# A branch ahead of expert 0, small loads in the first mixer, a shorter routing chain and MLP products on the unscaled residual

## The chip, the cores and the metric

One core of a Trainium2 chip runs one launch. The metric is the device time of that launch in microseconds, the median of several runs. Engines are called PE (TensorE), DVE (VectorE), ACT (ScalarE), POOL (GpSimd) and SP (the sync engine, which issues the DMAs of the weights).

## What is computed

256 tokens of 1024 features go through two blocks, all in float32. The first block is a gMLP and HGRN2 mixer and a mixture of 32 experts with two per token. The second block is modulated by a condition vector (12 modulation vectors of 1024, from `w_ada`), and holds an attention, an MLP, a differential attention and a second MLP.

```python
def first_block(x, ...):
    n1 = rms_norm(h, norm1_gain[l]); proj = n1 @ w_in[l]
    ...
    h = h + jnp.concatenate([a_out, b_out], axis=-1) @ w_out[l]
    n2 = rms_norm(h, norm2_gain[l])
    h = h + hier_moe(n2, ...)         # top-1 of 4 groups, then top-2 of its 8 experts
    return rms_norm(h, final_gain)
# an expert: silu(xb @ w_gate[e]) * (xb @ w_up[e]), times w_down[e]

def second_block(x, c, ...):
    cond = jax.nn.silu(c)
    for i in range(2):
        sh1, sc1, g1, sh2, sc2, g2 = jnp.split(cond @ w_ada[i] + b_ada[i], 6, axis=-1)
        h = rms_norm_2(x, ln_mix_g[i]) * (1.0 + sc1) + sh1
        y = nsa_mixer(h, ...) if i == 0 else diff_mixer(h, ...)
        x = x + g1 * y
        h = rms_norm_2(x, ln_mlp_g[i]) * (1.0 + sc2) + sh2
        x = x + g2 * (jnp.square(jax.nn.relu(h @ w_mlp_in[i])) @ w_mlp_out[i])
    return x
```

## The kernel before

Activations stay in SBUF, features on partitions: `res` is `[128, 8, 256]`. Weights stream once from HBM in tiles of 1 MB that SP issues in a fixed order through a ring of buffers; during the experts 18 tiles are in flight. An SP issue waits until the buffer that it fills has been read for the last time, and everything behind it on SP waits too. Outside the experts a float32 product is three passes of matmuls over a high and a low part (`passes`); for each half of a weight tile ACT writes the high part `whi` (L147) and DVE the low part `wlo` (L148). A scheduler orders the instructions of each engine by its own cost estimates, so that the order in the program is only loosely the order on an engine.

**Routing.** After the first mixer `lps` (the router's products) and `yps` (the tokens in natural layout, for the gather) come off PE. A chain of some twenty short DVE instructions yields the choice of experts `sel` (L1080), PE counts ranks from it (`pps`, L1107), DVE makes a one-hot matrix (`hot`, L1267), and PE gathers the tokens of the first four experts with it (`gps`, L1284). `natural` (L1083) writes the high and low parts of the natural tokens: for the first half of the features ACT writes the high part and a copy, and POOL subtracts (L1095); for the second half DVE does the low part behind the one-hot (L1098). Meanwhile PE works on tiles of `w_ada` (`adaps`, L183). `rint` (L1141) says how many tokens did not fit an expert's 64 slots; `past_slots` (L1186 to L1189) loads it into a register of each engine and branches over the block that handles them, which these inputs skip. It is called after expert 5.

**Experts.** Each is `gups` (gate and up, L1330), `htps`, `dps` (down, L1360), and `sums` (L1378) for two at a time. At e == 8 the program builds tables for the second block (L1434 to L1566), with 13 small DMAs on SP: `posi`, five `rg`, two `w`, `bgate`, and four `lv`.

**MLPs.** `out_late` ends the attention before: its `closing` (L476) adds four pairs of `olate` banks to `res`, and `Stats` (L285) counts squares on PE (`ssps`), 1 / rms follows through POOL (`rs_r`, L282) and is spread over partitions (`rbps`). `modulated` then writes the normalized, modulated `hT_hi` and `hT_lo` (L352 to L359); tiles of `w_ada` fill PE's waits there. `mlp` (L1658) runs nine steps j; PE does `hp` (96 matmuls of the first product) of step j and `mlp` (96 of the second) of the step before. `ada_vector` (L252, L254) does tiles of `w_ada` on DVE instead, two instructions a tile, 12 tiles during MLP 0.

Of the kernel before, what the change touches and what calls it, by code (L numbers as in the profile page):

```python
# [13 lines left out]
F32 = mybir.dt.float32  # L14
# [12 lines left out]
T = 256  # L27
D = 1024
# [9 lines left out]
BORROW = 13  # L38
IDLE = 8
# [3 lines left out]
def block_kernel(ctx: ExitStack, tc: tile.TileContext, A: dict, out: bass.AP):  # L43
# [21 lines left out]
    hT_hi = const.tile([P, KD, T], F32R, name="hT_hi")  # L65
    hT_lo = const.tile([P, KD, T], F32R, name="hT_lo")

# [5 lines left out]
    ones = const.tile([P, P], F32, name="ones")  # L73
# [211 lines left out]
    class Stats:  # L285


        def __init__(self, weights=None):
            self.w = weights
            self.q = {}  # L290
            self.tiles = None
# [10 lines left out]
        def square(self, pr, v):  # L302
            q = sc((P, 2, T), name="sq")
            self.q[pr] = q
            if pr == KD // 2 - 1 and self.w is None:
# [4 lines left out]
            if pr == KD // 2 - 1:  # L310
                hold(act=ins)
            if self.w is None:
                nc.vector.tensor_tensor(q[:, 0, :], q[:, 0, :], q[:, 1, :], op=ALU.add)

        def count(self, pr):
# [3 lines left out]
            n = 1 if self.w is None and pr < KD // 2 - 1 else 2  # L319
# [11 lines left out]
        def rstd(self):  # L331
# [7 lines left out]
            return rb[:, 0:T]  # L339

# [38 lines left out]


# [9 lines left out]
    def proj_T_steps(w, c0, outs, n=512, cut=1):  # L390

        for k0, t in colblock(w, c0, n, cut):
            for k1, hi, lo in halves(t):
                for kk in range(hi.shape[1]):
                    k = k0 + k1 + kk
                    for h in range(n // P):
                        for i, (a, b) in enumerate(passes((hi, lo), (hT_hi, hT_lo))):
# [5 lines left out]
                                stop=(k == KD - 1 and i == 2 and h % 2 == 1),  # L403
                            )
# [71 lines left out]
    def closing(banks, gate=None, st=None, each=None):  # L476
# [62 lines left out]
    def out_late(w, r0, got, gate=None, st=None, each=None):  # L539
# [4 lines left out]
        rows(w, r0 // P + 2, banks, got(2), 2, False, closing(banks, gate, st, each))  # L544
# [49 lines left out]
    with tc.tile_pool(name="pa", bufs=1, reuse_waits="tile") as pa:  # L594
# [90 lines left out]
        for h in range(2):  # L685
            small_loads.append(
                (g2[:, 4 * h : 4 * h + 4], A["norm2_gain"][:, h * 512 : (h + 1) * 512].rearrange("o (p k) -> (o p) k", k=4))
            )
        fT = [acc((P, 2, T), name="fT") for _ in range(2)]
# [316 lines left out]
    with (  # L1006
# [78 lines left out]
        def natural(h, behind=None):  # L1085
            s = slice(h * 512, (h + 1) * 512)
            for m in range(2):
# [3 lines left out]
                nc.scalar.activation(hi, ps, AF.Copy, scale=r2[:, m : m + 1])  # L1091
                if behind is None:
                    y = sc((P, 4, P), name="y")
                    nc.scalar.activation(y, ps, AF.Copy, scale=r2[:, m : m + 1])
                    nc.gpsimd.tensor_tensor(lo, y, hi.bitcast(F32), op=ALU.subtract)  # L1095
                else:
                    with tc.issue_after(behind.ins):
                        nc.vector.scalar_tensor_tensor(  # L1098
                            lo, ps, r2[:, m : m + 1], hi.bitcast(F32), op0=ALU.mult, op1=ALU.subtract
                        )  # L1100

        natural(0)
# [1162 lines left out]
```

## Time and profile before

| | |
|---|---|
| median of three runs | 1322.52 us (1319.78 to 1324.54) |
| profiled execution | 1326.57 us, of which the span from first to last instruction is 1324.8 |
| PE busy | 1279.0 us of the span |
| DVE, ACT, POOL busy | 637.6, 494.1, 72.2 us |
| mean granted clock of PE | 0.987 |

The span falls into the first mixer (to about 131 us), routing (to 148), experts (to about 611), the second block's attention (to 796), MLP 0 (to about 992), the differential attention (to 1127) and MLP 1. In the experts the DMA engines are busy throughout; in the rest it is PE. A view by windows gives for each stretch PE's granted clock as a share of full speed, the DMA engines' busy share and what they moved.

### The profile page before, as it was taken

To read this page: it belongs to the slowest core of one execution; us is meant where nothing else is said; L and a number is where in the kernel's file an instruction comes from. 1 tells how busy PE (TensorE), PEld (TensorE's weight loads), DVE (VectorE), ACT (ScalarE), POOL (GpSimd) and SP (SyncE) were. 2 spreads that over 40 slices of the span, in tenths; PEclk is the share of its full clock that TensorE was granted. 3 is DMA by queue.
4 is the path that set the end of the run, shared out by engine and by line. 5 is a ranking of instruction groups with operands and counts; after the bars stand their busy time and mean duration, and the time that the engine had idled before them with its cause. 6 is when DMAs were issued, how large, how long until landed. Compare 5 with 4: busy or idle time off the path is not lost.

```text
span 1324.8 us, 22820 instructions
## 1 busy us (share of the span) xinstructions
PE 1279.0 (97%) x9551; PEld 1010.1 (76%) x9551; DVE 637.6 (48%) x1172; ACT 494.1 (37%) x856; POOL 72.2 (5%) x95
## 2 busy tenths in 40 slices
PE   8999898999999999999999999999999999999998
PEld 7779565665555555556886688999997779999998
DVE  6865410131101111005786768667557677655554
ACT  6643310121101111004455644444445554544543
POOL 1010100000000000000410000000001220000000
PEclk9999899999999999998998999999999999999999
DMA  8997799899999999999545838688558432755520
GB/s 279 397 371 274 303 420 417 316 386 419 420 418 419 420 419 419 419 418 333 200 162 189 313 96 325 225 287 307 180 179 278 147 116 96 262 184 191 181 75 33
DMA packets 99157, 373.98 MB, mean 282 GB/s; under 512 B 10650, under 2 KB 14443, under 8 KB 74731
## 3 DMA queue, kind: packets, MB, share of 16 engines
q1 hardware_dynamic: 99050, 372.49, 74.2%
q8 instruction: 77, 1.26, 0.4%
q14 instruction: 30, 0.24, 0.0%
HBM read 371.41 MB, written 1.05 MB: 281 GB/s over the span
## 4 chain that ended last, share of the span: by engine, by line
PE 66%; issue 13%; DVE 2%; DMA 1%; ACT 1%; POOL 1%; POOLq 0%; DVEq 0%; ACTq 0%
PE mlp L441 14%; PE hp L398 13%; PE gups L1330 9%; PE dps L419 5%; PE dps L1360 4%; PE sums L1378 2%; PE oearly L527 2%; PE qp L419 2%; PE gps L1284 2%; PE adaps L183 2%; PE kv L419 1%; PE opair L2028 1%; PE kcv L419 1%; PE ptps L2019 1%; PE olate L441 1%
## 5 line engine op out<-in xcount | busy, mean ns | idle before, releaser
L148 DVE TENSOR_TENSOR wlo<-w,whi 128x1024 fp32r<-128x1024 f32 (+1 forms) x222 | 270.1, 1218 | 173.5 <-ACT whi L147 172.3
L147 ACT CAST whi<-w 128x1024 fp32r<-128x1024 f32 (+1 forms) x222 | 230.5, 1043 | 246.6 <-PE mlp L441 80.2
L1330 PE MATMUL gups<-w,xg 128*64 128x256 f32 x2048 | 236.4, 385 | 3.4 <-PEq L1189 3.4
L1330 PEld LDWEIGHTS gups<-w,xg 128*64 128x64 f32 x2048 | 145.5, 138 | 92.1 <-issue 25.9
L441 PE MATMUL mlp<-hid,whi 128*128 128x256 f32 x1024 | 183.9, 282 | 0.0
L441 PEld LDWEIGHTS mlp<-hid,whi 128*128 128x128 f32 x1024 | 156.8, 188 | 1.2 <-issue 1.2
L398 PE MATMUL hp<-hT_lo,whi 128*128 128x256 f32 x512 | 143.5, 283 | 1.1 <-DVE hT_lo L359 1.0
L441 PE MATMUL mlp<-hid,wlo 128*128 128x256 f32 x512 | 142.7, 282 | 0.0
L398 PE MATMUL hp<-hT_hi,wlo 128*128 128x256 f32 x512 | 141.4, 282 | 0.0
L398 PE MATMUL hp<-hT_hi,whi 128*128 128x256 f32 x512 | 140.7, 282 | 0.0
L1342 DVE TENSOR_TENSOR h<-h,gups 128x256 f32<-128x256 f32 x32 | 13.5, 422 | 248.8 <-ACT h L1341 248.8
L1360 PE MATMUL dps<-w,hT 128*64 128x512 f32 x496 | 113.2, 596 | 6.1 <-ACT hT L1350 5.0
L398 PEld LDWEIGHTS hp<-hT_lo,whi 128*128 128x128 f32 x512 | 96.0, 188 | 1.5 <-DVE hT_lo L359 1.4
L398 PEld LDWEIGHTS hp<-hT_hi,whi 128*128 128x128 f32 x512 | 95.4, 189 | 0.8 <-ACT hT_hi L358 0.8
L441 PEld LDWEIGHTS mlp<-hid,wlo 128*128 128x128 f32 x512 | 95.9, 188 | 0.0
L398 PEld LDWEIGHTS hp<-hT_hi,wlo 128*128 128x128 f32 x512 | 95.5, 188 | 0.0
L1360 PEld LDWEIGHTS dps<-w,hT 128*64 128x64 f32 x496 | 33.9, 137 | 65.7 <-issue 53.3
L1341 ACT ACTIVATE h<-gups 128x256 f32<-128x256 f32 x32 | 12.3, 383 | 179.4 <-PE gups L1330 179.4
L1371 DVE COPY ysb<-dps 64x512 f32<-64x512 f32 x31 | 21.2, 683 | 108.2 <-PE dps L1360 108.1
L1372 ACT COPY ysb<-dps 64x512 f32<-64x512 f32 x31 | 18.0, 581 | 140.0 <-DVE ysb L1371 140.0
L1378 PE MATMUL sums<-sw,ysb 128*128 128x256 f32 x256 | 61.5, 385 | 6.3 <-DVE ysb L1371 6.3
L282 POOL TENSOR_TENSOR rs_r<-rs_t,mhalf 128x8 f32<-128x8 f32 (+2 forms) x24 | 37.4, 1562 | 480.9 <-DVE rs_t L276 475.9
(529 smaller groups left out, 2019.1 us busy)
## 6 DMA issues: line engine op xcount, KB each, us to landing
w<-in_w_gate_dram SPq DMA_DIRECT2D x64, 1024.0 KB
w<-in_w_up_dram SPq DMA_DIRECT2D x64, 1024.0 KB
w<-in_w_down_dram SPq DMA_DIRECT2D x62, 1024.0 KB
w<-in_w_ada_dram SPq DMA_DIRECT2D x48, 1024.0 KB
w<-in_w_mlp_in_dram SPq DMA_DIRECT2D x32, 1024.0 KB
w<-in_w_mlp_out_dram SPq DMA_DIRECT2D x32, 1024.0 KB
w<-in_diff_w_in_dram SPq DMA_DIRECT2D x12, 1024.0 KB
w<-in_w_in_dram SPq DMA_DIRECT2D x10, 1024.0 KB
```

The source lines that it names most:

```text
L147: nc.scalar.copy(hi, v)
L148: nc.vector.tensor_tensor(lo, v, hi.bitcast(F32), op=ALU.subtract)
L183: nc.tensor.matmul(ps[32 * j : 32 * j + 32, :], lhsT, w[:, j * T : (j + 1) * T], start=start, stop=stop)
L282: nc.gpsimd.tensor_tensor(r, t, m, op=ALU.pow)
L398: nc.tensor.matmul(outs[h // 2][:, h % 2, :], a[:, kk, h * P : (h + 1) * P], b[:, k, :], start=(k == 0 and i == 0 and h % 2 == 0), stop=(k ...
L419: nc.tensor.matmul(outs[m], b[:, k, m * P : (m + 1) * P], a[:, kk, :], start=(k == 0 and i == 0), stop=(k == KD - 1 and i == 2),)
L441: nc.tensor.matmul(outs[dc // 2][:, dc % 2, :], a[:, 0, dc * P : (dc + 1) * P], b[:, a0 + kk, :], start=(first and kk == 0 and i == 0 and ...
L527: nc.tensor.matmul(banks[h // 2][:, h % 2, :], a[:, kk, h * P : (h + 1) * P], b[:, k, :], start=(k == 0 and i == 0 and h % 2 == 0), stop=( ...
L1284: nc.tensor.matmul(ps[:, j, :], part[:, m, k * P : (k + 1) * P], hot[:, m].rearrange("p e s -> p (e s)"), start=(n == 0), stop=(n == 3),)
L1330: nc.tensor.matmul(ps[j * 64 : (j + 1) * 64, s * 256 : (s + 1) * 256], xg[:, k, s0 : s0 + SLOTS], w[k // 4][:, k % 4, j * 256 : (j + 1) * ...
L1360: nc.tensor.matmul(dps[half * 64 : (half + 1) * 64, :], hT[:, c, j * 64 : (j + 1) * 64], dt[f // 2][:, f % 2, half * 512 : (half + 1) * 51 ...
L1378: nc.tensor.matmul(sums[k // 2][:, k % 2, :], t[:, k * P : (k + 1) * P], sw, start=(pr == 0 and k % 2 == 0), stop=(after is not None and k ...
```

## The change

Four parts. (1) `past_slots()` is called ahead of expert 0, and `weigh(0)` after the first products of expert 0. (2) Nine of the small loads go to the first mixer's list of small loads, and the four of `lv` with their four small instructions behind `out_late` of the second block's attention; the mask `cmask` is held once. (3) All high parts of the natural tokens are written first, on ACT, all low parts on DVE behind the one-hot; five bf16 matmuls of 128x512 whose result nobody reads run on PE ahead of `pps` and three behind. (4) The MLPs' first products run on `res * gain` without 1 / rms, written in `closing` pair by pair; a column 256 holds the shift, so that its product is the bias; each result takes 1 / rms (`rb`, the same for all partitions) and bias afterwards. `hp` is now four banks of 258 columns a step. Of the 36 tiles of `w_ada` on PE eight go to DVE, which does vectors 6 to 10.

```diff
@@ Stats
+        def scale(self):
+
+            r = rstd_of(self.ps[:, :, 0], D, "n")
+            rb = mm(name="rbps")
+            spread(r, rb[:, 0:T])
+            t = small.tile([P, T], F32, tag="nf", name="rb", bufs=3)
+            nc.scalar.copy(t, rb[:, 0:T])
+            return t
...
+    def feeding(gain, bias):
+
+        hi, lo = hX
+        for t in hX:
+            nc.vector.memset(t.bitcast(F32)[:, :, T + 1 : TX], 0.0)
+        b = bias[:, :, None]
+        nc.vector.tensor_copy(hi[:, :, T : T + 1], b)
+        nc.vector.tensor_tensor(lo[:, :, T : T + 1], b, hi[:, :, T : T + 1].bitcast(F32), op=ALU.subtract)
+
+        def feed(pr):
+            for k in (2 * pr, 2 * pr + 1):
+                g = gain[:, k : k + 1]
+                nc.scalar.activation(hi[:, k, 0:T], res[:, k, :], AF.Copy, scale=g)
+                nc.vector.scalar_tensor_tensor(
+                    lo[:, k, 0:T], res[:, k, :], g, hi[:, k, 0:T].bitcast(F32), op0=ALU.mult, op1=ALU.subtract
+                )
+
+        return feed
...
+    def proj_X_steps(w, c0, outs):
+
+        for k0, t in colblock(w, c0, 512):
+            for k1, hi, lo in halves(t):
+                for kk in range(hi.shape[1]):
+                    k = k0 + k1 + kk
+                    for h in range(4):
+                        for i, (a, b) in enumerate(passes((hi, lo), hX)):
+                            nc.tensor.matmul(
+                                outs[h],
+                                a[:, kk, h * P : (h + 1) * P],
+                                b[:, k, :],
...
@@ closing
+            if feed is not None:
+                feed(pr)
+                st.square(pr, v)
+                if pr >= 2:
+                    st.count(pr - 2)
+                return
...
@@ first mixer
+        posi = const.tile([P, 2], I32, name="posi")
+        small_loads.append((posi, A["positions_2"].rearrange("o (m p) -> p (o m)", p=P)))
...
+            small_loads.append((rope_gains[:, i, :], g[:, 0:16].to_broadcast([P, 16])))
...
@@ routing
-        natural(0)
+        for h in range(2):
+            natural(h, "high")
         for _ in range(2):
             ada_half([route["last"]])
+
+        unread = mm(name="unread")
+
+        def busy(n):
+            for _ in range(n):
+                nc.tensor.matmul(
+                    unread, onesb, onesb[:, None, :].to_broadcast([P, 4, P]), start=True, stop=True
+                )
+
+        with tc.manual_schedule(engines={mybir.EngineType.PE}):
+            busy(WAIT)
...
+        with tc.issue_after(ranked.ins):
+            busy(3)
...
             if q4 == 0:
-                natural(1, one_hot)
+                for h in range(2):
+                    natural(h, "low", one_hot)
...
         wt, rint = token_weights()
-        weigh(0, hot0)
+        past_slots()
...
                 h, silu, prod = gate_up(e)
+                if e == 0:
+                    weigh(0, hot0)
...
-            if e == 5:
-                past_slots()
...
@@ mlp
-                hp = [mm((P, 2, T), name="hp") for _ in range(2)]
-                proj_T(w_i, j * 512, hp)
+                hp = [(mm if j else acc)((P, TX), name="hp") for _ in range(4)]
+                for n, _ in enumerate(proj_X_steps(w_i, j * 512, hp)):
+                    if j == 0 and n == 3:
+                        st.count(2)
+                        st.count(3)
+                        rb = st.scale()
...
-                    nc.scalar.activation(r, hp[i], AF.Relu)
+                    b = pw.tile([P, 4], F32, tag="nm", name="hb")
+                    for c in range(2):
+                        nc.vector.tensor_copy(b[:, c : c + 1], hp[2 * i + c][:, T : T + 1])
+                        nc.vector.tensor_tensor(r[:, c, :], hp[2 * i + c][:, 0:T], rb, op=ALU.mult)
+                        nc.scalar.activation(r[:, c, :], r[:, c, :], AF.Relu, bias=b[:, c : c + 1])
...
-                    nc.vector.tensor_tensor(r, r, r, op=ALU.mult)
+                    nc.scalar.activation(r, r, AF.Square)
...
-                if ada_at[0] < vectors:
-                    ada_vector(ada_sum)
+                for _ in range(2):
+                    if j and ada_at[0] < vectors:
+                        ada_vector(ada_sum)
...
@@ second block, after the first mixer
-    out_late(w_o, 512, late, mods[2], st)
-    modulated(st, 0, 3, col("lnm", 0, 8))
-    st = Stats()
-    mlp(0, lambda banks: closing(banks, mods[5], st), 10)
+    st_x = Stats(plain=True)
+    out_late(w_o, 512, late, mods[2], st_x, feed=feeding(*modulation(0, 3, col("lnm", 0, 8))))
...
+        nc.sync.dma_start(lv[:, i, :], A[f"diff_{nme}_2"].to_broadcast([P, 64]))
...
+    mlp(0, lambda banks: closing(banks, mods[5], st), st_x, 11)
```

The order of instructions, at three places. First PE between the gather for the first four experts and expert 0. Before:

```order
L1284 MATMUL gps<-hot,hT_lo 128x256 x3
L1284 MATMUL gps<-hot,hT_hi 128x256 x2
L1284 MATMUL gps<-hot,hT_lo 128x256 x2
L1137 MATMUL rps<-ident,rmx 1x128
L1313 MATMUL wps<-ident,hw 128x128 x4
L1330 MATMUL gups<-w,xg 64x256 x64
L1348 MATMUL htps<-ident,h 128x128 x2
L1360 MATMUL dps<-w,hT 64x512 x8
```

After, up to the branch, and then from behind the skipped block:

```order
L1367 MATMUL gps<-hot,hT_lo 128x256 x2
L1219 MATMUL rps<-ident,rmx 1x128
L1270 TENSOR_LOAD rint
L1271 COMPARE_AND_BRANCH
L358 MATMUL rbps<-ident,rs_r 128x128 x2
L1287 COMPARE_AND_BRANCH
L1287 UNCONDITIONAL_BRANCH x2
L2342 BRANCH_PREFETCH_HINT
```

```order
L1287 UNCONDITIONAL_BRANCH
L1271 UNCONDITIONAL_BRANCH
L1413 MATMUL gups<-w,xg 64x256 x32
L1396 MATMUL wps<-ident,hw 128x128 x4
L1413 MATMUL gups<-w,xg 64x256 x32
L1431 MATMUL htps<-ident,h 128x128 x2
L1443 MATMUL dps<-w,hT 64x512 x8
```

Behind `rps` PE now loads the register and branches, and the `wps` of `weigh(0)` stand after the first half of `gups`.

Second, SP's queue. Before, behind the skipped block (its end is the first three rows) in the experts:

```order
L1189 UNCONDITIONAL_BRANCH
L127 DMA w<-in_w_down_dram 128x2048
L1453 DMA posi<-in_positions_dram 128x2x1
L1483 DMA rg<-in_nsa_q_gain_dram 128x16
L1483 DMA rg<-in_nsa_k_gain_dram 128x16 x2
L1483 DMA rg<-in_diff_q_gain_dram 128x16
L1516 DMA w_2646<-in_nsa_w_ck_2_dram 128x64
L1517 DMA w_2646<-in_nsa_w_cv_2_dram 128x64
L1560 DMA bgate<-in_nsa_b_gate_dram 128x48
L127 DMA w<-in_w_gate_dram 128x2048 x2
L127 DMA w<-in_w_up_dram 128x2048 x2
```

After, in the first mixer, and behind the skipped block, which now ends ahead of most of the experts' loads:

```order
L105 DMA g_107<-in_norm_gain_dram 128x4 x2
L105 DMA posi<-in_positions_dram 128x2x1
L105 DMA rope_gains<-in_nsa_q_gain_dram 128x16
L105 DMA rope_gains<-in_nsa_k_gain_dram 128x16 x2
L105 DMA rope_gains<-in_diff_q_gain_dram 128x16
L105 DMA rope_gains<-in_diff_k_gain_dram 128x16
L105 DMA w_200<-in_nsa_w_ck_2_dram 128x64
L105 DMA w_200<-in_nsa_w_cv_2_dram 128x64
L105 DMA bgate<-in_nsa_b_gate_dram 128x48
L131 DMA w<-in_w_in_dram 128x4x512 x2
L131 DMA w<-in_w_ada_dram 128x2x1024 x2
L131 DMA w<-in_w_in_dram 128x4x512 x2
```

```order
L1287 UNCONDITIONAL_BRANCH
L1271 UNCONDITIONAL_BRANCH
L1270 ISA x2
L131 DMA w<-in_w_up_dram 128x2048 x2
L131 DMA w<-in_w_down_dram 128x2048 x2
L131 DMA w<-in_w_gate_dram 128x2048 x2
L131 DMA w<-in_w_up_dram 128x2048 x2
```

The small loads stand in front of the first mixer's weights instead of the experts' weights.

Third, PE where the second block's attention ends and MLP 0 begins. Before:

```order
L441 MATMUL olate<-oT,whi 128x256 x2
L441 MATMUL olate<-oT,wlo 128x256
L323 MATMUL ssps<-ones,sq 128x1 x4
L183 MATMUL adaps<-w,cond 32x256 x8
L323 MATMUL ssps<-ones,sq 128x1 x4
L183 MATMUL adaps<-w,cond 32x256 x8
L344 MATMUL rbps<-ident,rs_r 128x128 x2
L183 MATMUL adaps<-w,cond 32x256 x16
L398 MATMUL hp<-hT_hi,whi 128x256 x2
L398 MATMUL hp<-hT_lo,whi 128x256
```

After:

```order
L448 MATMUL hp<-hT_hi,whi 128x258 x2
L328 MATMUL ssps<-ones,sq 128x1 x4
L491 MATMUL olate<-oT,whi 128x256 x2
L491 MATMUL olate<-oT,wlo 128x256
L491 MATMUL olate<-oT,whi 128x256 x2
L491 MATMUL olate<-oT,wlo 128x256
L491 MATMUL olate<-oT,whi 128x256 x2
L491 MATMUL olate<-oT,wlo 128x256
L491 MATMUL olate<-oT,whi 128x256 x2
L491 MATMUL olate<-oT,wlo 128x256
L448 MATMUL hp<-hT_lo,whi 128x258
L448 MATMUL hp<-hT_hi,wlo 128x258
```

The `adaps` and the wait for `rbps` between the last `olate` and `hp` are gone; `hp` begins while `olate` still runs.

## Rows read from the trace of the kernel before

**Rows 1.** Windows: length, busy us of PE, PEld, DVE, ACT, POOL; clock, DMA share, GB/s.

```profile
90.00:135.00 45.00, 43.18 (x359) 38.76 (x358) 25.05 (x42) 13.59 (x22) 3.20 (x8) 1.00 0.70 265
...
140.00:145.00 5.00, 4.21 (x20) 4.24 (x21) 3.59 (x13) 0.47 (x1) 0.00 (x0) 0.50 0.97 406
145.00:150.00 5.00, 4.83 (x35) 3.89 (x36) 3.08 (x10) 2.71 (x4) 1.66 (x2) 0.83 0.00 0
...
235.00:250.00 15.00, 14.49 (x116) 9.68 (x113) 4.38 (x10) 3.23 (x7) 1.04 (x1) 1.00 0.58 198
285.00:295.00 10.00, 10.00 (x90) 7.49 (x87) 2.04 (x4) 1.92 (x4) 0.00 (x0) 1.00 0.79 310
300.00:580.00 280.00, 272.43 (x1916) 158.89 (x1912) 34.51 (x70) 35.22 (x76) 3.12 (x3) 1.00 1.01 419
```

**Rows 2.** Chain that ended last, 220 to 300 us: start, us, what.

```profile
226.02 10.10 PE gups L1330 x64
236.11 4.03 PE gps L1284 x32
...
244.96 6.91 PE gups L1330 x64
```

**Rows 3.** Line view of the branch, L1189: duration ns min/median/max, start us; who waited.

```profile
L1189 PEldq COMPARE_BRANCH  x1: 6006/6006/6006, 219.6 to 219.6; - x1
...
  PE gups L1330: 3.4, 1
```

**Rows 4.** SP's waits, 215 to 245 us: total us, times, longest.

```profile
SPq L1189 <- SPq L1189: 14.5, 2, 12.0
```

**Rows 5.** Timeline, routing to expert 0: start us, us, instruction [idle before <-releaser].

```profile
137.81 1.26 POOL L1095 TENSOR_TENSOR hT_lo<-y,hT_hi 128x512 fp32r<-128x512 f32 x1
137.98 1.31 DVE L1070 TENSOR_TENSOR hot<-iota,eidx 128x64 f32<-128x64 f32 x2
...
139.69 0.20 PE L1107 MATMUL pps<-sel,lower 128*128 128x32 bf16 x2 [2.56 <-DVE sel L1080]
140.79 1.41 PE L1284 MATMUL gps<-hot,hT_hi 128*128 128x256 f32 x5 [0.87 <-DVE hot L1267]
140.89 1.40 DVE L1098 SCALAR_TENSOR_TENSOR hT_lo<-yps,rs_r,hT_hi 128x512 fp32r<-128x512 f32 x2
...
148.33 3.03 PE L1330 MATMUL gups<-w,xg 128*64 128x256 f32 x26
148.41 0.13 DVE L1141 CAST rint<-rtop 1x1 int32<-1x1 f32 x1
150.32 0.33 SPq L127 DMA_DIRECT2D w<-in_w_up_dram  x1
```

**Rows 6.** Timeline of SP at the small loads among the experts.

```profile
239.59 0.83 SPq L1483 DMA_DIRECT2D rg<-in_nsa_k_gain_dram  x2
```

**Rows 7.** Timeline of PE around the starts of the two MLPs.

```profile
796.46 0.95 PE L323 MATMUL ssps<-ones,sq 128*128 128x1 f32 x8
...
1126.95 0.95 PE L323 MATMUL ssps<-ones,sq 128*128 128x1 f32 x8
```

**Rows 8.** Chain that ended last, in the MLPs.

```profile
829.22 11.39 PE mlp L441 x96
840.62 11.50 PE hp L398 x96
...
1134.39 23.24 PE hp L398 x192
```

**Rows 9.** Groups by form, 796 to 1010 us: busy us, mean ns, idle before.

```profile
L254 DVE SCALAR_TENSOR_TENSOR adasum<-w,cond,adasum 128x1024 f32<-128x1024 f32 x20 | 25.6, 1280 | 1.9 <-DMA w<-in_w_ada_dram 1.9
L183 PE MATMUL adaps<-adasum,ones 128*32 128x256 f32 x24 | 1.9, 391 | 0.0
```

**Rows 10.** Windows in MLP 0, with columns as in Rows 1.

```profile
900.00:920.00 20.00, 20.00 (x170) 20.00 (x170) 19.48 (x20) 8.21 (x11) 0.00 (x0) 1.00 0.90 324
920.00:940.00 20.00, 20.00 (x170) 20.00 (x169) 10.91 (x11) 9.48 (x11) 0.00 (x0) 1.00 0.72 251
```

More of the change, by code (lines that the diff above doesn't have):

```diff
@@ L27 @@
 T = 256
+TX = T + 2
 D = 1024
@@ L38 @@
 BORROW = 13
+WAIT = 5
 IDLE = 8
@@ L64, in block_kernel @@
     res = const.tile([P, KD, T], F32, name="res")
-    hT_hi = const.tile([P, KD, T], F32R, name="hT_hi")
-    hT_lo = const.tile([P, KD, T], F32R, name="hT_lo")
+    hT = [const.tile([P, KD * TX], F32R, name=f"hT_{n}") for n in ("hi", "lo")]
+    hT_hi, hT_lo = (t[:, : KD * T].rearrange("p (k t) -> p k t", t=T) for t in hT)
+    hX = [t.rearrange("p (k t) -> p k t", t=TX) for t in hT]
     ident = const.tile([P, P], F32, name="ident")
@@ L72, in block_kernel @@
     nc.vector.memset(mhalf, -0.5)
-    ones = const.tile([P, P], F32, name="ones")
+    ones = const.tile([P, 32], F32, name="ones")
     nc.vector.memset(ones, 1.0)
@@ L285, in block_kernel, with __init__ @@
     class Stats:
-        def __init__(self, weights=None):
+        def __init__(self, weights=None, plain=False):
             self.w = weights
+            self.plain = plain
             self.q = {}
@@ L304, in square @@
             self.q[pr] = q
-            if pr == KD // 2 - 1 and self.w is None:
+            if pr == KD // 2 - 1 and self.w is None and not self.plain:
                 for j in range(2):
@@ L309, in square @@
             ins = nc.scalar.activation(q, v, AF.Square)
-            if pr == KD // 2 - 1:
+            if pr == KD // 2 - 1 and not self.plain:
                 hold(act=ins)
-            if self.w is None:
+            if self.w is None and not self.plain:
                 nc.vector.tensor_tensor(q[:, 0, :], q[:, 0, :], q[:, 1, :], op=ALU.add)
@@ L318, in count @@
             q = self.q.pop(pr)
-            n = 1 if self.w is None and pr < KD // 2 - 1 else 2
+            n = 1 if self.w is None and pr < KD // 2 - 1 and not self.plain else 2
             for j in range(n):
@@ L403, in proj_T_steps @@
                                 stop=(k == KD - 1 and i == 2 and h % 2 == 1),
+                            )
+                    yield
+    def proj_X_steps(w, c0, outs):
[9 more added lines that the diff above has]
+                                b[:, k, :],
+                                start=(k == 0 and i == 0),
+                                stop=(k == KD - 1 and i == 2),
                             )
@@ L543, in out_late @@
         rows(w, r0 // P, banks, got(0), 0, True)
-        rows(w, r0 // P + 2, banks, got(2), 2, False, closing(banks, gate, st, each))
+        rows(w, r0 // P + 2, banks, got(2), 2, False, closing(banks, gate, st, each, feed))
     class Chains:
@@ L1083, in block_kernel, with natural @@
         y_lo = hT_lo.rearrange("p k t -> p (k t)").rearrange("p (m d) -> p m d", m=2)
-        def natural(h, behind=None):
+        def natural(h, part, behind=None):
             s = slice(h * 512, (h + 1) * 512)
@@ L1108, in block_kernel @@
             if m == 1:
-                nc.tensor.matmul(pps[:, m, 0:NE], onesb, sel[:, 0, :], start=False, stop=True)
+                ranked = nc.tensor.matmul(pps[:, m, 0:NE], onesb, sel[:, 0, :], start=False, stop=True)
+        with tc.issue_after(ranked.ins):
+            busy(3)
         rank = bt("rank", (P, 2, NE))
@@ L1656, in weights_T, with mlp @@
         return t
-    def mlp(lay, close, vectors=0):
-        if vectors:
-            ada_sum = ct("adasum", (P, D), tag="klo")
-            if ada_at[1]:
-                ada_half()
+    def mlp(lay, close, st, vectors):
+        ada_sum = ct("adasum", (P, D), tag="klo")
+        if ada_at[1]:
+            ada_half()
         w_i, w_o = A["w_mlp_in_2"][lay], A["w_mlp_out_2"][lay]
-        banks = [acc((P, 2, T), name="mlp") for _ in range(4)]
         pend = None
@@ L2231, in result @@
         )
-    mlp(1, lambda banks: closing(banks, mods[11], each=result))
+    mlp(1, lambda banks: closing(banks, mods[11], each=result), st, 12)
 _INS = [
```

96 lines of the change are left out of this document (47 added, 49 removed).

## The prediction

> **What bounds the kernel now.** I read the windows first. From 300 to 580 us the DMA engines are full at 419 GB/s, while PE is busy 272.4 of 280 us [rows 1]. So the experts are bound by the stream of weights, with PE close behind: it has 7.6 us to spare in 280, or some 12 over the 445 us in which experts run. Time comes out of this stage only where the stream stands still, and the windows show where: 145 to 150 us moves nothing, 235 to 250 runs at 198 GB/s, and 285 to 295 at 310. The view of waits names the second: SP stood 12.0 us behind its own branch [rows 4], and the small loads followed. PE too waited 3.4 us at the branch, whose fetch shows as an instruction of 6.0 us [rows 3], and then did 64 `gups` in 10.10 us instead of 6.91 [rows 2]. The reader is to see there a PE that was idle and came back slow.
>
> The first gap is the start of the experts: all buffers are full, and the next issue, at 150.32, has to wait for `gups` of expert 0, from 148.33 [rows 5]. Ahead of that PE waits 2.56 us for `sel`, and the gather then runs from 140.79 to about 147.3, at a granted clock of 0.50, the lower level of 1.2 GHz, in 140 to 145 [rows 1, 5]; the same 32 matmuls take 4.03 later [rows 2].
>
> In the MLPs PE is the bound: 96 `hp` take 11.50 us and 96 `mlp` 11.39, back to back [rows 8]. Only the starts lose time. In MLP 0 the last `olate` has been sent at 796.46 and the first 192 `hp` end at 829.22: 32.8 us against 2 x 11.50 of work, 9.8 lost. In MLP 1 it is 1134.39 + 23.24 - 1126.95 = 30.7, so 7.7 lost [rows 7, 8].
>
> **Part 1 and 2, the stalls of the stream.** Against 419 GB/s the stream loses 15 x (1 - 198/419) = 7.9 us at the branch and its small loads, and 10 x (1 - 310/419) = 2.6 at `rg` and `lv`: 10.5 us that go, if nothing replaces them [rows 1].
>
> What the loads cost where they go: an issue takes 0.83/2 = 0.42 us [rows 6], nine of them 3.8 us of SP. In the first mixer SP runs ahead of PE: from 90 to 135 us the DMA share is only 0.70, about 13 us of slack in which SP waits for buffers [rows 1]. That work hides them, so I take 0, and 3.8 as the bound. The four of `lv` stand in SP's queue in front of weights and a tile of `w_ada` in MLP 0, and a multiply of theirs waits for them on DVE with `wlo` behind it; this goes under part 4.
>
> What the branch costs in its new place is the largest unknown. It now stands on the path from `rint` to expert 0, on PE, SP and all others, with `gups` behind it on PE and the refill issues on SP. I work out the start. The POOL subtraction at 137.81 lies over two DVE instructions of 128x64 that take 1.31 us together, and another such pair stands just before [rows 5]. Without POOL's work I take 2.0 us off `sel`, between 0 and the 2.56 that PE waits. With PE kept busy by the eight unread matmuls I expect the clock to hold, so that the gather takes 4.03 instead of 6.5: 2.5 less. Against that all four low parts now stand on DVE behind the one-hot, two more at 1.40/2 = 0.70 each [rows 5], and the gather needs them: 1.4, and 0.2 for the fillers. `rint` is ready 2.9 earlier, at 145.6 instead of 148.5. Then the register load, about 0.5, and the fetch: between 0 and PE's 6.0 [rows 3]; I take 2.5, nearer the lower end, because 145 to 150 moves nothing [rows 1], whereas at 219.6 the fetch stood in a full stream. Expert 0 would start at 148.6, as before (148.33).
>
> But PE then has some 4 us without work, more than the 3.4 us behind which it ran 64 `gups` in 10.10. I expect the same slow start, and so the first release, 150.32 - 148.33 = 2.0 us after the start before, to come twice as late: the stream starts 0.3 + 2.0, say 2.5 us later. Bounds: 2 earlier (no fetch, clock kept), and 8 later, if SP's fetch takes 12.0 us again [rows 4] from 146.1.
>
> The Trainium skill, Runtime: NRT & Kernel Launch, section Instruction fetch mechanics, says that a taken branch to a target outside the two pages held has to fetch the target's page by DMA before the engine goes on; it gives no time. By that rule the stall is moved and not removed, as the first rival has it; the rows of the branch agree that there is a fetch.
>
> So the stream gains 10.5 - 2.5 = 8.0 us. PE's 12 us of spare hold that only barely, after a slow start that takes 3 of them, and I take 1 off: **7.0 us**, between 2.5 and 10.
>
> **Part 3** is counted in this start.
>
> **Part 4, the MLPs' starts.** `adaps` and the wait for 1 / rms leave the space between `olate` and `hp`. What stays of the 7.7 us in MLP 1: the counting matmuls, 8 in 0.95 us [rows 7] and 32 of them now, 3.8; spreading, 0.7; and a wait of some 1.5 for the fourth `olate` bank, which `hp` now needs at once, of which about 1 lies under matmuls: an estimate of 5.0, between 3 and 7. Gain 2.7. In MLP 0 the same, 9.8 - 5.0 = 4.8, less 2 (0 to 4) for DVE, where the multiply of `lv` and an `ada` instruction wait for DMAs ahead of `wlo`: 2.8.
>
> Added to PE: 258 columns for 256 make 11.50 into 11.59, 0.09 x 16 steps = 1.4 us. Two more vectors on DVE add their strips on PE, 24 matmuls in 1.9 us for three vectors [rows 9], so 0.64 each: 1.3, or 2.4 with the gaps around them. The eight `ada` tiles that leave PE are in the lost time above and not counted twice.
>
> Added to DVE: eight tiles of two instructions at 1.28 us [rows 9]. In MLP 0 a stretch with `ada` tiles has DVE busy 19.48 of 20 us and PE never waits; one without has 10.91 [rows 10]. A step of 22.9 us then needs 10.91 x 22.9/20 = 12.5, three tiles 7.7, and about 1 for the four short copies and the 258 columns' scaling (an estimate; the four multiplications by `rb` have the elements of the two squares that go to ACT): 21.2 of 22.9. It fits, with 1.7 to spare, so 0. The cover is the weights' low parts that DVE has written ahead; if it is gone the cost is in the second rival.
>
> Part 4 sums to 2.7 + 2.8 - 1.4 - 1.3 = **2.8 us**, between -4 and 7.
>
> **Sum.** 7.0 + 2.8 = 9.8 us. The profiled execution of 1326.57 (span 1324.8) would become 1316.8; it lies 4.05 above the median of the runs, and against 1322.52 the forecast is 1312.7.
>
> **Rivals.** *The branch eats what it frees.* SP fetches for 12 us again, which starts the stream 8 late, and the MLPs give little because the counting and DVE's queue take the place of `adaps`: 10.5 - 8 + 0 = 2.5, so 1320.0, no change. For it speaks that the branch now stands on every engine's path where it had stood behind 18 loaded tiles; against it that the DMA engines are empty there.
>
> *DVE becomes the bound in MLP 0.* It ends slower than before. The place is `wlo` behind `ada` tiles that wait for their DMA, and behind the scaling that waits for `hp`. The spare of 1.7 us a step decides: if waits of DVE exceed it, one tile of 2.56 a step shows on PE, in six steps 15.4 us: 1312.7 + 15.4 = 1328.1. For it speaks 19.48 of 20 us; against it that PE was never late there.
>
> *All of it works.* The clock holds through the branch and the fetch is short, 10 us; the starts of the MLPs lose 2 us each instead of 5 and 7: 2.8 + 8 = 10.8, capped by the fourth bank's wait at about 8. 1322.5 - 18 = 1304.5. For it speaks the idle DMA; against it the 10.10 us behind a shorter idle time.
>
> **How the numbers follow.** Forecast, with its bounds near (1307 to 1318): 0.55. All of it works: 0.15. Branch eats it: 0.18. DVE late: 0.12. The measurement can tell 0.3%, about 4 us; so faster (below 1318.5) 0.70, same 0.18, slower (above 1326.5) 0.12. The range leaves out most of the slow case and the far end of the best: 1305 to 1322.
>
> **What would show it.** Right: after 235 us no window below 410 GB/s until the experts end; PE's wait of 2.56 for `sel` under 1; a granted clock near 1 in the gather; `hp` beginning under `olate`, and 192 of them ending some 28 to 30 us behind the last `olate`. The clock in the first 10 us of expert 0 tells whether the slow start came with the branch. Wrong: SP's first refill beyond 155 us, or PE waiting for `wlo` in MLP 0.

## The result

| | median us | range | ratio to before |
|---|---|---|---|
| before | 1322.4 | 1319.78 to 1324.54 | |
| changed | 1307.3 | 1305.44 to 1309.14 | 0.989 (0.9869 to 0.9911) |

The kernel is 15.1 us faster; forecast were 9.8. The profiled execution took 1306.74 us, span 1305.0, mean granted clock 0.995. It lies 0.6 below its median, while that of before lay 4.2 above its own, so the two traces differ by 19.8. From landmarks of both traces (start of expert 0, last `dps` of the experts, end of the last `olate`, first `mlp`, start of the last `mlp` of MLP 0):

| stretch | before us | after us | difference |
|---|---|---|---|
| to `gups` of expert 0 | 148.33 | 145.70 | -2.6 |
| experts, to the last `dps` | 459.41 | 452.67 | -6.7 |
| second block's attention | 188.72 | 188.28 | -0.4 |
| start of MLP 0 | 32.76 | 25.89 | -6.9 |
| steps of MLP 0 | 164.19 | 166.47 | +2.3 |
| differential attention | 133.54 | 133.69 | +0.1 |
| start of MLP 1 | 30.68 | 25.88 | -4.8 |
| rest | 167.17 | 166.42 | -0.7 |

Of the 2.6 us in the first row 1.1 lie ahead of the routing, in the first mixer: the router's last product (`lps`) ends at 130.66 instead of 131.78. From there to the first `gups` it takes 15.0 us instead of 16.5.

The busy times and one costly group of the page after:

```profile
PE 1263.6 (97%) x9471; PEld 1001.2 (77%) x9471; DVE 652.6 (50%) x1268; ACT 512.6 (39%) x918; POOL 68.4 (5%) x92
...
L1413 PE MATMUL gups<-w,xg 128*64 128x256 f32 x2048 | 233.7, 381 | 3.8 <-PEq L1271 2.8
```

The windows after, in the columns of [rows 1]:

```profile
140.00:145.00 5.00, 2.90 (x25) 2.59 (x23) 3.89 (x16) 2.07 (x5) 0.00 (x0) 1.00 0.76 315
145.00:150.00 5.00, 3.32 (x29) 2.54 (x31) 0.76 (x2) 1.11 (x1) 1.04 (x1) 1.00 0.05 10
235.00:250.00 15.00, 15.00 (x104) 9.11 (x102) 1.10 (x2) 1.34 (x3) 0.05 (x1) 1.00 1.01 420
285.00:295.00 10.00, 9.48 (x70) 6.47 (x71) 4.38 (x10) 3.06 (x7) 1.04 (x1) 1.00 1.01 419
300.00:580.00 280.00, 271.65 (x1892) 157.94 (x1889) 34.78 (x70) 34.30 (x76) 3.12 (x3) 1.00 1.01 421
```

Both dips of [rows 1] are filled, 198 and 310 GB/s have become 420 and 419, and the gather's clock is 1.00 instead of 0.50. The chain of waits after, where expert 0 starts (start us, us, what):

```profile
145.40 0.30 issue
145.70 1.91 PE gups L1413 x15
147.61 0.98 issue
148.59 5.56 PE gups L1413 x49
```

Here 64 `gups` end 8.45 us after they began, against 10.10 behind the old branch [rows 2]; in this trace their first 15 run at the full rate and the rest follow a pause of 0.98, in which PE waited for nothing that the profile shows.

### The profile page after: what moved, and what is told of

The parts are those of the page before. It is cut to its first block, busy times and chain, and to the rows that moved or that the text cites. A ratio compares the mean times of both kernels' runs of the same rounds, so it can differ in the third digit from the quotient of the medians.

```text
span 1305.0 us, 22821 instructions
## 1 busy us (share of the span) xinstructions
PE 1263.6 (97%) x9471; PEld 1001.2 (77%) x9471; DVE 652.6 (50%) x1268; ACT 512.6 (39%) x918; POOL 68.4 (5%) x92
## 3 DMA queue, kind: packets, MB, share of 16 engines
q8 instruction: 76, 1.25, 0.4%
## 4 chain that ended last, share of the span: by engine, by line
PE 74%; issue 11%; DVE 2%; ACT 1%; POOL 0%; DVEq 0%; ACTq 0%; POOLq 0%
PE hp L448 14%; PE mlp L491 14%; PE gups L1413 12%; PE dps L1443 6%; PE dps L469 5%; PE sums L1461 3%; PE gps L1367 2%; PE oearly L584 2%; PE qp L469 2%; PE olate L491 2%; PE adaps L187 1%; PE kv L469 1%; PE opair L2098 1%; PE kcv L469 1%; PE ptps L2089 1%
## 5 line engine op out<-in xcount | busy, mean ns | idle before, releaser
L1413 PE MATMUL gups<-w,xg 128*64 128x256 f32 x2048 | 233.7, 381 | 3.8 <-PEq L1271 2.8
L448 PE MATMUL hp<-hT_lo,whi 128*128 128x258 f32 x512 | 144.0, 282 | 0.0
L448 PE MATMUL hp<-hT_hi,whi 128*128 128x258 f32 x512 | 143.7, 283 | 0.0
L448 PE MATMUL hp<-hT_hi,wlo 128*128 128x258 f32 x512 | 142.5, 282 | 0.0
L1454 DVE COPY ysb<-dps 64x512 f32<-64x512 f32 x31 | 21.2, 683 | 107.1 <-PE dps L1443 107.0
```

The costliest lines, as they stand in the source:

```text
L448: nc.tensor.matmul(outs[h], a[:, kk, h * P : (h + 1) * P], b[:, k, :], start=(k == 0 and i == 0), stop=(k == KD - 1 and i == 2),)
L1413: nc.tensor.matmul(ps[j * 64 : (j + 1) * 64, s * 256 : (s + 1) * 256], xg[:, k, s0 : s0 + SLOTS], w[k // 4][:, k % 4, j * 256 : (j + 1) * ...
L1454: nc.vector.tensor_copy(t[e2 * 64 : e2 * 64 + 64, 0:512], dps[0:64, :])
```

## The experiments

All times are medians; differences are to the kernel before. The last column is the mean granted clock of the runs, and it proved useful: within the runs of one kernel, over 85 runs of twelve builds, the time rises by 0.9 us for each 0.001 that this clock is lower (correlation -0.77).

| run | median us | ratio | to before | clock |
|---|---|---|---|---|
| before (24, 17, 7 and 7 runs) | 1322.2 to 1322.8 | | | 0.990 |
| changed / again (`e9_after_again`) | 1307.3 / 1307.3 | 0.989 (0.9869 to 0.9911) / 0.9883 (0.9867 to 0.99) | -15.1 / -15.2 | 0.9935 / 0.993 |
| `e1_branch_only` | 1320.65 | 0.9988 (0.9974 to 1.0002) | -1.6 | 0.991 |
| `e2_loads_only` | 1316.91 | 0.9961 (0.9945 to 0.9977) | -5.3 | 0.989 |
| `e3_chain_only` | 1321.15 | 0.9994 (0.9981 to 1.0006) | -1.1 | 0.991 |
| `e4_mlp_only` | 1316.61 | 0.9953 (0.9937 to 0.9969) | -5.6 | 0.989 |
| `e5_before_shifted` | 1319.03 | 0.9981 (0.9968 to 0.9993) | -3.1 | 0.989 |
| `e6_after_shifted` | 1310.13 | 0.991 (0.9895 to 0.9926) | -12.0 | 0.991 |
| `e7_no_fillers` | 1306.68 | 0.9883 (0.9866 to 0.99) | -15.5 | 0.993 |
| `e8_branch_behind` | 1310.41 | 0.9911 (0.9896 to 0.9925) | -11.8 | 0.992 |
| `e10_branch_late` | 1309.58 | 0.9903 (0.9884 to 0.9922) | -12.9 | 0.993 |
| `e11_dve_load` | 1309.35 | 0.9901 (0.9884 to 0.9918) | -13.1 | 0.992 |
| `e12_shift64` | 1310.70 | 0.9911 (0.9895 to 0.9928) | -12.1 | 0.991 |

### Each part alone on the kernel before

The edits are the parts of the diff above. The `ones` tile is 32 columns wide instead of 128 in the runs of parts 2 and 4, and the five and three unread matmuls belong to part 3.

> The kernel before with only the branch moved ahead of expert 0. Two theories of the expert stage. Stream: its end is set by the weights, so that a stall counts by the bytes it costs; the branch's share of the dip at 235 to 250 us goes (about 5 of the 7.9 us, the small loads stay there), and a later start gives 1 to 2 back: 3 to 4 us faster, and the last w_down is still the last thing that PE waits for. PE: its end is set by PE, which at the branch waited 3.4 us and then ran 64 gups 3.2 us slower; these 6.6 go and a wait of some 2 to 3 us ahead of expert 0 comes: 3.5 to 4.5 us faster if the clock holds there, 0 to 1 if it falls as it did at the old place. Both are near in the time; the trace parts them: from the first gups to the last dps, PE theory 452 to 453 us (before 459.4) whatever the small loads do, stream theory 455 or more.

> The kernel before with only the nine small loads moved to the first mixer and the four of lv behind the attention (the constant of ones is 32 columns wide to make room; nothing reads the rest). Stream theory: the dips of 2.6 us at 285 to 295 and of some 3 at 238 to 244 go: 4 to 6 us faster. PE theory: nothing, within 1 us, since the windows fill up but PE never waited for them; from the first gups to the last dps stays at 459 us.

> The kernel before with only the shorter routing chain. The start of expert 0 comes 2.5 to 3 us earlier (the trace of the changed kernel has routing to rint 3.4 us shorter), and stream and PE both start earlier with it: 2 to 3 us faster by either theory. If the clock in the gather does not hold without the rest, 0 to 1.

> The kernel before with only the MLPs' part. By the prediction's terms 2.8 us faster (-4 to 7). By the trace of the changed kernel both starts lose 3.0 us instead of 9.8 and 7.7, the steps of MLP 0 grow by 2.2 and those of MLP 1 shrink by 0.7: 10 us faster.

The four differences add up to -13.6, near the -15.1 of the whole, but not for the expected reasons, and parts 1 and 3 alone cannot be told from none. With part 1 alone the dip at the branch loses less and yet the experts do not gain from it. Its windows:

```profile
235.00:250.00 15.00, 14.48 (x114) 9.41 (x113) 3.95 (x9) 3.01 (x7) 1.04 (x1) 1.00 0.79 292
285.00:295.00 10.00, 9.56 (x84) 7.50 (x80) 2.86 (x7) 2.63 (x6) 0.06 (x1) 1.00 0.90 355
```

By the prediction's own formula the stream still loses 15 x (1 - 292/419) + 10 x (1 - 355/419) = 6.1 us there, 4.4 less than before. From `gups` of expert 0 to the last `dps` it took 454.7 us, between the two expectations (452 to 453, and 455 or more). Without the wait at the branch and the slow `gups` behind it, it took 452.8, as before (452.8). Over all traces but that of `e8_branch_behind` this remainder is 452.2 on average (451.3 to 452.8) where the loads stand in the experts (five traces: before, e1, e3, e4, e5) and 450.8 (449.7 to 451.2) where they do not (eight). So 10.5 us of dips are worth about 1.5 us. With part 2 alone the whole stretch took 456.2 us, not the 459 that I had expected if PE sets it.

Where the rest went is told by the ends of the two queues. Loads of `w_down` on SP and the last matmul of the experts on PE, in the trace before:

```profile
582.84 9.26 SPq L1166 DMA_DIRECT2D w<-in_w_down_dram  x4
607.74 1.08 PE L1397 MATMUL dps<-w,hT 128*64 128x256 f32 x8
```

and after:

```profile
571.28 5.15 SPq L1248 DMA_DIRECT2D w<-in_w_down_dram  x2
598.37 1.08 PE L1480 MATMUL dps<-w,hT 128*64 128x256 f32 x8
```

The last issue ends at 576.43 instead of 592.10, 15.7 us earlier; PE ends only 9.4 earlier. PE's waits from 160 to 590 us, before (total us, times, longest):

```profile
PE sums L1378 <- DVE ysb L1371: 6.3, 8, 0.8
PE dps L1360 <- ACT hT L1350: 5.0, 10, 0.5
PE gups L1330 <- PEq L1189: 3.4, 1, 3.4
PE dps L1360 <- DMA w<-in_w_down_dram: 1.1, 2, 0.6
```

After, only the first two stay, with the same numbers. PE waited 1.1 us for weights in the whole stage: the experts were bound by PE and its two chains over DVE and ACT, and the full DMA engines ran ahead into buffers.

My expectation for part 4 alone was wrong too: 10 us, and 5.6 came (4.1 to 8.3 by the interval). In its trace the starts and steps of the MLPs, counted from the matmuls' own starts and ends (25.9, 167.5, 25.9 and 167.4 us, where before has 32.4, 164.6, 30.4 and 167.4), are together 8.1 shorter. About 1 of the rest is the runs' clock by the slope above; what remains is open.

### The same kernel at other places in SBUF

Part 2 gave -5.3 us although the missing dips are worth about 1.5, and in its MLPs many groups of 96 `hp` took 11.26 us, which that part does not touch. The narrower `ones` tile had moved all later buffers. These two runs move buffers and nothing else; the added tile is written once and never read. The edit of the first, of which the second (on the changed kernel) has the `spare` lines alone, with 32 columns:

```diff
-    ones = const.tile([P, P], F32, name="ones")
+    ones = const.tile([P, 32], F32, name="ones")
+    spare = const.tile([P, 16], F32, name="spare")
     nc.vector.memset(ones, 1.0)
+    nc.vector.memset(spare, 0.0)
```

> The kernel before, with only its buffers shifted: the constant of ones is 32 columns wide and a spare of 64 bytes stands behind it, so that the weights' halves lie 320 bytes lower in SBUF, where they lay in the kernel with only the loads moved. Nothing else changes. Theory of place: there the 96 matmuls of hp took 11.26 us instead of 11.50, because of the place; they do so here, 2.5 to 3.5 us faster in all, and of the 5.3 us of the loads' move 2 or so are left for the loads themselves. Rival: the pace came with the loads or the order of work; hp stays at 11.50, no change.

> The changed kernel, with a spare of 128 bytes that shifts the weights' halves to the same offset from a multiple of 256 bytes as in the shifted kernel before. Theory of place: hp with 258 columns goes from 11.46 to 11.35 us (11.26 + 0.09), 16 times, 1.5 to 2 us faster than the changed kernel, about 1305.5. Rival: no change, 1307.3.

In the first of them the chain in MLP 1 has, beside some pieces of 11.39:

```profile
1161.71 11.26 PE hp L400 x96
```

where before has 11.50 [rows 8] to 11.52, and the kernel is 3.1 us faster (0.9968 to 0.9993) with the same instructions but for the write of the spare tile; in the traces its MLPs' starts and steps are together 3.2 shorter. So some 3 of the 5.3 us of part 2 are the place, and about 2 the loads. The second failed my expectation: `hp` took 11.48 and not 11.35. The last run moves the changed kernel's buffers by 64 bytes a partition and leaves out the unread matmuls:

```diff
     ones = const.tile([P, 32], F32, name="ones")
+    spare = const.tile([P, 16], F32, name="spare")
...
-            busy(WAIT)
+            pass
...
-        with tc.issue_after(ranked.ins):
-            busy(3)
```

> The changed kernel without the unread matmuls of the routing, and with 64 unread bytes a partition ahead of the MLPs' weight halves, so that these start at 160 instead of 96 bytes above a multiple of 256. Place theory (the pace of hp follows where the stationary halves lie): hp x96 leaves 11.46 us, to somewhere between 11.35 and 11.60, with mlp x96 still 11.39, and the time moves with it by 16 times the difference, up to 2.2 us around 1306.7. Rival (the earlier differences came from the other buffers that moved along, or from the chip of the day): hp x96 stays at 11.46 and the time within 0.6 us of 1306.7.

Its chain in MLP 1:

```profile
1171.40 11.53 PE hp L450 x96
1182.93 11.39 PE mlp L493 x96
```

With 258 columns, 96 `hp` thus mostly take 11.46 (changed), 11.48, 11.53 and, in part 4 alone, 11.59 us, with the weights' halves at 96, 224, 160 and 32 bytes above a multiple of 256; `mlp` takes 11.38 to 11.40 everywhere. The pace follows the place, but which buffer's place was not separated, and the rule is open. Of the 3.4 us by which this run is slower than the changed kernel (4.0 against `e7_no_fillers`, from which the shift alone parts it), 0.7 is this pace by the traces' starts and steps of the MLPs, where I had expected 0.07 x 16 = 1.1; its clock, 0.991 against 0.9935, would be 2.2 by the slope above. The same slope gives 2.1 of the 2.8 us of the second run. In which stretch their clock falls is open, since the profiled executions (1305.63 us in the last run) do not show it.

### The branch at three places

```diff
-        past_slots()
...
                 h, silu, prod = gate_up(e)
                 if e == 0:
+                    past_slots()
                     weigh(0, hot0)
```

> The changed kernel with the branch behind the first products of expert 0 instead of ahead of them. PE does not wait for rint any more, so expert 0 starts 2 to 2.8 us earlier; the branch stands where the refill of the stream has begun. If the price of a branch is the fetch in a busy stream: PE's branch takes some 3 to 6 us instead of 0.64, 1 to 4 us slower than the changed kernel. If the stream of two tiles does not hold the fetch up: under 1 us, and 1 to 2 us faster.

`e10_branch_late` puts `past_slots()` back behind expert 5 and `weigh(0)` ahead of expert 0; all else is the changed kernel.

> The changed kernel as it is, beside the next two on the same chip: 1306 to 1309.

> The changed kernel with the branch back behind expert 5 (and the weights of expert 0 ahead of its products), the other three parts kept. PE theory: PE waits 3.4 us there and runs 64 gups 3 us slower, against 2.8 us of waiting that go ahead of expert 0: 3 to 4.5 us slower than the changed kernel, and from the first gups to the last dps, less the wait and the slow stretch, 451 to 452 us as in the other kernels, though the stream loses some 4 us at 235 to 250. Stream theory: that loss of 4 comes on top, 6 to 8 slower.

The line view of the branch, of the changed kernel (duration ns min/median/max, start us; who waited, us):

```profile
L1271 SPq COMPARE_BRANCH  x1: 54/54/54, 144.6 to 144.6; - x1
...
L1271 PEldq COMPARE_BRANCH  x1: 642/642/642, 144.6 to 144.6; - x1
...
  PE gups L1413: 2.8, 1
```

and of the branch behind the first products:

```profile
L1271 PEldq COMPARE_BRANCH  x1: 5692/5692/5692, 148.4 to 148.4; - x1
...
  PE wps L1396: 4.4, 1
```

The same branch takes 0.64 us on PE where the window around it moves 10 GB/s, 5.7 where the refill of the buffers is under way, and 6.0 in the full stream [rows 3]. Over all traces it takes 0.45 to 1.30 us on PE ahead of expert 0 (seven traces) and 5.7 to 6.2 at the other two places (seven). SP's own waits inside the branch (total us, times, longest), in the changed kernel and behind the first products, against 14.5 in the full stream [rows 4]:

```profile
SPq L1271 <- SPq L1271: 1.1, 2, 0.7
...
SPq L1271 <- SPq L1271: 7.8, 4, 3.4
```

The Trainium skill, Runtime: NRT & Kernel Launch, section Instruction fetch mechanics, states that a taken branch to a page that is not held waits for a DMA that fetches it. The seven long branches agree: inside each lies one transfer of 16 KB on the instruction queue. The row of the kernel before, from 219.6 to 225.6 us (packets, MB, share):

```profile
q8 instruction: 1, 0.02, 1.2%
```

This transfer begins at 223.1 us, 3.5 behind the start of the branch, while weights move. But inside none of the seven short branches lies a transfer on that queue. So the price goes with the place, and with the load on the DMA queues there; whether a fetch with empty queues is that cheap, or PE had nothing to fetch ahead of expert 0, no run separates.

Around the branch PE loses 3.4 us of wait and 10.10 - 6.91 = 3.2 at the old place, 2.8 and 8.45 - 6.91 = 1.5 at the new. So part 1 is worth 2.3 in these traces, 0.7 in those of `e10_branch_late` (3.5 and 1.7) and `e9_after_again` (2.6 and 1.9), and by medians 1.6 (alone) to 2.3 (1309.58 - 1307.28), less than the 3 to 4.5 that I had expected of `e10_branch_late`. PE's wait itself is little shorter at the new place: until `rint` is there 1.1 us pass behind the gather, and the register load takes 0.5, ahead of the 0.64 of the branch.

The slow `gups` go with the clock. One window behind the branch each, of the kernel before and of `e9_after_again`:

```profile
226.00:236.00 10.00, 9.98 (x64) 6.45 (x64) 0.00 (x0) 0.00 (x0) 0.00 (x0) 0.70 0.92 375
150.00:155.00 5.00, 5.00 (x38) 3.77 (x36) 0.22 (x1) 0.00 (x0) 0.00 (x0) 0.76 0.34 98
```

Before, the granted clock is at half from 225.2 to 232.1 us. With the branch ahead of expert 0 it falls for a shorter time in five of seven traces (in `e9_after_again` from 149.0 to 152.4), and 64 `gups` take 8.6 to 8.8; in those of the changed kernel and of `e12_shift64` it stays at 1.00.

Behind the first products the branch was 3.1 us slower than in the changed kernel. SP stood long there, and the remainder of the experts was 451.9 us, 1.1 above the mean of the eight traces: little of the stream's loss showed. In `e10_branch_late` the stream loses more than 4 us by the prediction's formula,

```profile
230.00:235.00 5.00, 5.00 (x44) 4.30 (x41) 1.39 (x3) 1.53 (x4) 0.00 (x0) 1.00 0.36 151
235.00:240.00 5.00, 4.50 (x29) 2.26 (x29) 2.30 (x6) 1.13 (x3) 1.04 (x1) 1.00 0.88 326
```

and its remainder is 450.7, as in the kernels without that loss.

### Without the unread matmuls

The edit is that of `e12_shift64` without its spare tile.

> The changed kernel without the eight unread matmuls in the routing. If they hold the clock: PE waits some 1.3 us for sel and more for the one-hot, the granted clock falls to 0.5 in the gather, which takes 6 us instead of 4.5; expert 0 starts 1.5 to 2.5 us later and the time is 1 to 2.5 us longer. Rival: the wait is now too short for the clock to fall (sel comes two us earlier anyway); the same time, within 0.5.

One window over the gather, 138 to 143 us, of the changed kernel:

```profile
138.00:143.00 5.00, 4.67 (x33) 4.03 (x33) 4.89 (x15) 1.60 (x4) 0.00 (x0) 1.00 1.02 428
```

and without the matmuls:

```profile
138.00:143.00 5.00, 4.76 (x24) 4.43 (x25) 4.22 (x11) 0.95 (x2) 0.00 (x0) 0.70 1.00 423
```

Here PE spends part of the gather at 1.2 GHz, the lower level, and from the last `lps` to expert 0 it takes 15.9 us, 0.9 more than in the changed kernel. But `e12_shift64` has no unread matmuls either, and its gather kept the clock:

```profile
139.00:144.00 5.00, 4.63 (x33) 4.03 (x33) 4.89 (x16) 1.52 (x5) 0.00 (x0) 1.00 1.02 429
```

So they are not always needed; with them the gather kept its clock in all seven traces. The median is the same within what can be measured (-0.6), not the 1 to 2.5 us longer that I had expected if they hold the clock.

### More work on DVE in MLP 0

```diff
+                for _ in range(4 if lay == 0 and j else 0):
+                    nc.vector.tensor_tensor(r, r, r, op=ALU.mult)
```

> The changed kernel with four more multiplications of 128x512 (0.69 us each, 2.7 us a step) on DVE in seven steps of MLP 0; they write only a buffer that is read no more. The rival of the prediction said that DVE has 1.7 us to spare in a step of three tiles. If that is so, steps with three tiles take 1 us more, others nothing: 2 to 5 us slower than the changed kernel in all, with PE waiting for wlo. If the low parts written ahead and the steps with fewer tiles even it out: under 1 us, and no waits for wlo.

The added multiplications are of dead values. Three of the six windows from 840 to 960, columns as in [rows 1]:

```profile
840.00:860.00 20.00, 20.00 (x173) 19.66 (x166) 19.48 (x21) 9.67 (x13) 0.00 (x0) 1.00 0.85 295
...
900.00:920.00 20.00, 20.00 (x169) 19.95 (x168) 18.83 (x27) 10.77 (x15) 0.00 (x0) 1.00 0.96 345
...
940.00:960.00 20.00, 20.00 (x170) 20.00 (x169) 19.53 (x28) 7.21 (x9) 0.00 (x0) 1.00 0.98 356
```

With up to 2.7 us more a step DVE is nearly full in these three (18.39, 17.79 and 15.48 of 20 in the others). PE is busy 20.00 of 20 in all six and waits for no `wlo`; MLP 0 with its start, to the end of its last `mlp`, takes 192.9 us, against 192.6. In the changed kernel DVE is busy 18.40, 18.13, 16.83 and 14.79 in the four windows from 840 to 920. The median is 2.1 higher, within the 2 to 5 that I had expected if DVE were the bound, but MLP 0 gives only 0.3 of it; the clock of these runs (0.992) would explain 1.2, and the rest is open.

## Why the prediction was right, and where it was not

**The sum held, the largest step did not.** "The experts are bound by the stream of weights, with PE close behind" was wrong. I had read the full DMA engines as the bound and PE's 7.6 idle us as spare; the view of PE's waits in that stretch, which I did not read, shows 1.1 us of waiting for weights. The sign that I had set for the stream came (no window of 10 us from 235 to 575 is below 417 GB/s), and yet the 10.5 us of dips were worth about 1.5. The term of 7.0 us was filled by other things: PE's loss at the old branch, counted by me only as a sign, and the shorter routing. In the trace routing and experts gave 9.3, of which 1.1 came ahead of the routing. That the forecast of 9.8 came near the 15.1 is to that extent luck.

**The branch.** I took 2.5 us of fetch between 0 and 6.0, nearer the lower end because the DMA engines are empty there. The value was too high: 0.64 on PE, and a wait of 2.8 in all. The reason is not shown: no transfer of instructions lies inside that branch, so PE may have had nothing to fetch. The slow start I took at 2.0 us; most traces with the branch there show it (64 `gups` in 8.6 to 8.8 us against 6.91, so 1.7 to 1.9: e1, e6, e7, e9, e11), that of the changed kernel has 1.5 without the clock's fall, 1.0 of it `issue`. The rival in which the branch eats what it frees falls: SP was not held for 12 us, and its first refill stands at 149.00, 1.3 earlier than before and not 2.5 later. The time lies nearer to the rival in which all works (1304.5), but the clock held through the branch, as that rival wants it, in only two of seven traces.

**The routing chain.** PE's 2.56 us for `sel` are gone, the gather takes 4.67 us at a clock of 1.00 where I took 4.03, and from the last `lps` to expert 0 it takes 1.5 us less instead of 0.3 more, the branch included (1.9 less with part 3 alone, 1.8 more with part 1 alone). The start by itself says less: in `e9_after_again`, the same kernel, expert 0 starts at 148.79, since the granted clock was at half from 12.5 to 19.3. Alone the part gave 1.1 us, less than the 2 to 3 that I had expected and within what cannot be told from none.

**The MLPs' starts.** The mechanism was right and the size off. The chain at MLP 1 after (start us, us, what):

```profile
1110.15 0.24 PE hp L448 x2
1110.39 0.79 PE ssps L328 x8
1111.17 1.53 PE olate L491 x12
1112.70 0.85 PE hp L448 x7
1113.56 0.79 PE ssps L328 x8
1114.34 1.19 PE hp L448 x9
1115.53 0.34 PE ssps L328 x4
1115.87 3.71 PE hp L448 x30
1119.57 1.23 PE ssps L328 x12
1120.80 4.40 PE hp L448 x36
1125.20 0.44 PE rbps L358 x4
1125.65 12.93 PE hp L448 x108
1138.58 11.40 PE mlp L491 x96
```

Behind the last `olate` (1112.70) stand 25.88 us: 2 x 11.46 of `hp`, and 3.0 lost, not 5.0: `ssps` 0.79 + 0.34 + 1.23 and `rbps` 0.44. A quarter of the counting already lay under `olate`, there was no wait for the fourth bank, and in MLP 0 no wait of DVE. So the gains were 6.9 and 4.8 us where I had 2.8 and 2.7. Against that MLP 0 lost 2.3 us in its steps, where I had 1.3 for strips and 0.7 for columns (half of 1.4). One step of MLP 0 after:

```profile
837.77 0.57 PE adaps L187 x8
838.34 3.76 PE mlp L491 x30
842.10 0.34 PE adasum L225 x4
842.44 5.57 PE mlp L491 x46
848.01 11.47 PE hp L448 x96
```

A vector adds 0.57 + 0.34 = 0.91 us, two make 1.8: between my 1.3 and my bound of 2.4. The columns cost 0.09 a step as worked out where the place is unchanged (part 4 alone, 11.59), and nothing in the changed kernel (11.46), whose buffers lie elsewhere. That is a gain for which the prediction had no term: the starts and steps of the MLPs take 385.0 us in the changed kernel and 386.6 in part 4 alone, 1.7 less.

**DVE as the bound** falls, by the run with more load. My count of 21.2 of 22.9 us a step was about right; that low parts written ahead carry steps that go beyond it is likely, but no run shows it by itself.

**Where the difference of 15.1 lies.** Part 4 alone 5.6, part 1 alone 1.6, part 2 about 2.2 (5.3 without the 3.1 of the place), part 3 alone 1.1, and the place of the buffers 1.7: 12.2. The rest of 2.9 lies within the intervals of the parts. The runs' clock, 0.9935 against 0.990, stands for about 3 us of it by the slope, no cause of its own beside the parts: 0.990 becomes 0.991 with part 1 or part 3 alone. In the trace before the clock is at half from 139.9 to 146.7 us (the gather, behind the waits that part 3 shortens [rows 5]) and from 225.2 to 232.1 (behind the branch); in the changed kernel's trace both are gone. How the 3 us divide was not settled.

**Not reproducible was the clock's fall itself.** In the trace before it is at half from 1092.2 to 1095.6 us, behind a wait of 1.25 us, and costs 1.6; the changed kernel, e1 and e2 have the same instructions and the same wait without it. This is part of the 4.2 us by which that trace lay above its median. The changed kernel's trace has a fall of its own in the same stretch, from 984.4 to 987.8, which `e9_after_again`, the same kernel, has not (133.4 us of differential attention against 131.8). So the +0.1 in the first table is two falls that cancel.

## What to carry to other kernels

Full DMA engines do not make a stage bound by its loads: read what PE waits for in that stage, and whether the last load or the last matmul ends earlier when the stream gets better. A taken branch can cost a tenth at another place: ahead of the first refill the instruction took 0.45 to 1.30 us on PE instead of 6. Look whether a transfer of instructions lies inside it and what else the DMA queues carry then, and count the wait for the value that it tests: here PE's wait fell only from 3.4 us to between 2.5 and 3.5. Before a gain of a few us is put down to an edit, move the buffers without the edit, compare the granted clock of the runs, and look at a second trace of the same kernel.

## What the hardware showed that I had not expected

The pace of some matmuls changed when nothing but the place of the buffers in SBUF did: 96 `hp` took 11.26 to 11.52 us with 256 columns and 11.46 to 11.59 with 258, as the tiles ahead of them in SBUF grew or shrank (by 64, 128 and 320 bytes a partition in the three runs made for it), while 96 `mlp` stayed at 11.38 to 11.40. In the kernel before, the shift alone gave 3.1 us, more than parts 1, 2 and 3 gave each in the sum above.

A taken branch took 0.45 to 1.30 us on PE with nearly idle DMA queues and no 16 KB of instructions fetched inside it, and 5.7 to 6.2 us with the refill or the full stream and one such transfer inside it; SP waited 1.1 us in it in the changed kernel, and 7.8 and 14.5 in the other two places.

The granted clock fell in one execution of the changed kernel and not in the other, at three places: in the first mixer and behind the branch in `e9_after_again` alone, and behind MLP 0 in the changed kernel's first trace alone.
